# A hybrid encoder block: the planner's prices for TensorE, and small products of two heads in alternation

## The chip, the cores and the metric

One core of a Trainium2 chip runs one transformer-like block on 1024 frames of 1024 channels in float32. The metric is device microseconds of that core for one execution. TensorE (PE) multiplies, VectorE (DVE) and ScalarE (ACT) do elementwise work and empty the PSUM banks, GpSimd (POOL) does little, SyncE (SP) issues every DMA.

## The reference, cut to what matters

```python
h = x
n1 = modulate(rms_norm(h, norm1_g), sh1, sc1)
h = h + 0.5 * g1 * swiglu(n1, ffn1_w1, ffn1_w3, ffn1_w2)
n2 = modulate(rms_norm(h, norm2_g), sh2, sc2)
proj = n2 @ w_in
y_rwkv = rwkv7_mixer(proj[..., :N_RWKV_COLS], ...)      # 8 heads of 64: a recurrent delta rule
y_attn = chunk_band_attention(...)                      # 8 heads of 64: 64-frame chunks, 9-chunk band
h = h + g2 * (concatenate([y_rwkv, y_attn]) @ w_out)
n3 = modulate(rms_norm(h, norm3_g), sh3, sc3)
h = h + 0.5 * g3 * swiglu(n3, ffn2_w1, ffn2_w3, ffn2_w2)
```

The nine vectors sh, sc, g come from `silu(c) @ w_ada + b_ada`. The mixer's in-context rate is `a = sigmoid(a0 + ad @ w_a_up)`, a product over 64 rows: the second product of the low-rank adapters.

## The kernel before, in words

The frames are worked in two halves of 512, A and B. The large products (both feed-forward blocks, the projection, the output projection) take float32 operands split into a high and a low part and make three products of 128 rows, 128 columns and 512 moving columns each, summed in one PSUM bank. Weights stream through `wst` (as they lie in memory), `whi` and `wlo` (high and low part). Tiles of the products are `mm` and `mmb`; the operands are `nh`, `nl` (normed input), `ah`, `al` (gated activations) and `mh`, `ml` (the mixers' outputs).

The order of all instructions is made in Python while the program is built, by a planner. Each stage is a generator that yields what it waits for; `drive` keeps a table of when each engine will be free and each tile ready (class `Clock`) and always resumes the first stage, by priority, that is ready at TensorE's planned time. `mm` and `tp_` (a transpose) tell the table the price `d` of each product on TensorE. On the chip every engine runs its list strictly in that order, and semaphores make it wait where a tile is not there yet. A 512-column product of split operands has the price `n / 2400 + 0.004`, so 0.2173 us; a float32 product of up to 64 columns has `n / 1200 + 0.012`.

The large stages are the mains, in this order of priority: f1A (first feed-forward of half A), pA (projection), oA (output projection), f1B, pB, oB, f2A, f2B. They fill TensorE between the links of the other stages: rA and rB (the recurrence), aA and aB (attention), the norms n1B, n2A, n2B, n3A, n3B, and mA, mB, which read the mixers' outputs back from memory (`mx`), split them and give oA and oB their input. oA waits for rA, aA and pA; pB waits for f1B and oA; n2B waits for f1B. The norms' row factors `rstd`, their `nv` tiles and the `mx` tiles share four buffers named `th`. PSUM has three banks for `mm` and five (pool `b`) for everything else, and a main may take one of the five only when two are free.

The recurrence takes two heads at a time (a pair), four pairs a half, in two groups of two. For each pair `rwkv1` makes the operands: `ap`, the adapter's second product (lines 1203 to 1209), over partitions 64 to 127 only; `gb`, for each head and each of 8 chunks a product of 64 rows by 128 columns by 128 moving columns; and `bt`, 8 transposes a head. Head 0 lies in partitions 0 to 63, head 1 in 64 to 127. All of head 0's `gb` come first, four chunks a bank, then all of head 1's, then `bt` of head 0, then `bt` of head 1. DVE turns each `gb` bank into `GA` and `GR` with a mask. A group's triangular blocks then go through memory to DVE (`inverse`), and `rwkv2` builds two sets of 32-row, 32-column products, `qb` and `ub`, 8 for head 0 and then 8 for head 1, before it walks the 8 chunks with the products `px`, `pu` and `pz`. The output products `yb` follow: first those with `GR`, head by head, then those with `RA` and `Z`, where the code before already alternates the heads, into two banks:

```python
        for c in range(NC):
            for h in range(2):
                s = slice(h * 64, h * 64 + 64)
                self.mm(out(h, c), RA[s, c, 0], Z[s, c], start=False, ...)
```

In the trace a float32 product shows as two matmul records and two weight loads, a transpose and a split-operand product as one of each.

Of the kernel before, what the change touches and what calls it, by code (L numbers as in the profile page):

```python
# [10 lines left out]
AF = mybir.ActivationFunctionType  # L11
# [5 lines left out]
P = 128  # L17
# [5 lines left out]
C = 64  # L23
NC = H // C
# [8 lines left out]
NEVER = 1e9  # L33
# [13 lines left out]
class Clock:  # L47

    SEM = 0.21

    def __init__(self):
        self.pe = 0.0
        self.at = dict(vector=0.0, scalar=0.0, gpsimd=0.0, sync=0.0, dma=0.0)
        self.base, self.wr, self.rd, self.by, self.left = {}, {}, {}, {}, {}
        self.new, self.live = set(), set()
        self.slots, self.psum = {}, set()
# [86 lines left out]
        for x in outs:  # L145
            self.write(x, e, eng)

    def matmul(self, out, ins, d):
        self.pe = max(self.pe, self.after(ins, [out], "pe")) + d
        for x in ins:  # L150
            self.read(x, self.pe + self.SEM)
        self.write(out, self.pe + self.SEM, "pe")

# [86 lines left out]
class Builder:  # L240
    def __init__(self, tc, a, es):
        self.tc, self.a, self.es = tc, a, es
        self.clock = Clock()
        self.nc = Core(tc.nc, self.clock)
        self.uid = 0
        self.tasks, self.mains = [], []
        self.n, self.ssq, self.tags = {}, {}, {}
        self.done, self.group = set(), None

    def nm(self, s):  # L250
        self.uid += 1
# [236 lines left out]
        return self.tile(self.pb, "b", 5, name, reads=reads)  # L488


    def mm(self, out, lhsT, rhs, start=True, stop=True, **kw):
        m, n = width(lhsT), width(rhs)
        if lhsT.dtype == F32R:
            d = n / 2400 + 0.004
        else:
            d = 2 * max(2 * n / 2400, m / 1200) if m > 64 else n / 1200 + 0.012
        self.clock.matmul(out, (lhsT, rhs), d)
        self.nc.tensor.matmul(out, lhsT, rhs, start=start, stop=stop, **kw)  # L498

    def tp_(self, out, in_, ident):  # L500
        self.clock.matmul(out, (in_,), 0.112 if in_.shape[0] > 64 else 0.058)
        self.nc.tensor.transpose(out, in_, ident)  # L502

    def colsum(self, out, x, h=1):
# [220 lines left out]
    def norm(self, key, hf, j, src=None):  # L725
        nc = self.nc
        s = self.sets[hf]
        if j == 0:
            d = 0
            for x in self.fetch(src):  # L730
                if x is None:
                    yield from self.sumsq(hf, j, d, self.fetched)
                    d += 1
                else:
                    yield x
        rstd = yield from self.root(hf, j)
        nh, nl, vs = [], [], []

        def scale(d):
            if j:  # L740
                return getattr(self, f"s{j}")[:, d : d + 1], self.mod[:, 3 * j - 2, d : d + 1]
            return tuple(self.n1m[v][d // 2][:, d % 2 : d % 2 + 1] for v in (1, 0))

        def low(d):
            nc.vector.scalar_tensor_tensor(nl[d], vs[d], scale(d)[1], nh[d].bitcast(F32), op0=OP.add, op1=OP.subtract)

        def step(d, x):
            yield x, rstd, "th", f"n{hf}", lambda: 0.0 if len(self.mains) < 2 else self.clock.at["vector"]
            sc, sh = scale(d)
            v = self.th("nv", 2)  # L750
            nc.vector.scalar_tensor_tensor(v, x, sc, rstd, op0=OP.mult, op1=OP.mult)
            vs.append(v)
            nh.append(self.tile(s, f"n{hf}", 16, "nh", dt=F32R))
            nl.append(self.tile(s, f"n{hf}", 16, "nl", dt=F32R))
            nc.scalar.activation(nh[d], v, AF.Identity, bias=sh)
            if d == 0:
                self.n[key] = nh, nl
            else:
                low(d - 1)

        if src is None:
            for d in range(ND):
                yield from step(d, self.h[hf][d])
                if j == 1:
                    self.free(self.h[hf][d])
        else:
            d = 0
            for x in self.fetch(src):
                if x is None:
                    yield from step(d, self.fetched)  # L770
                    d += 1
                else:
                    yield x
        yield nh[ND - 1]
        low(ND - 1)


    def place(self):
# [387 lines left out]
    def rwkv_prep(self, hf):  # L1166

        nc = self.nc
        lo = yield from self.shift(8, hf)
        gd = yield from self.shift(9, hf)  # L1170
        self.twd = self.tb(hf, "twd")
        self.tad = self.tb(hf, "tad")
        nc.gpsimd.memset(self.twd[64:65], 1.0)
        yield lo
        nc.scalar.activation(self.twd[0:64], lo[0:64], AF.Tanh)
        nc.vector.tensor_copy(self.tad[64:128], lo[64:128])
        self.sgd = self.tb(hf, "sgd")
        yield gd
        nc.scalar.activation(self.sgd, gd, AF.Tanh, scale=0.5)
        self.free(lo, gd)  # L1180
        yield self.sgd
        nc.vector.tensor_scalar(self.sgd, self.sgd, 0.5, 0.5, OP.mult, OP.add)

    def rwkv1(self, hf, p):

        nc = self.nc
        cs = slice(p * P, p * P + P)
        c3 = lambda t: t.rearrange("p (c t) -> p c t", c=NC)
# [3 lines left out]
        nc.sync.dma_start(wdu[0:64], self.a["w_decay_up"][:, cs])  # L1192
        nc.sync.dma_start(wdu[64:65], self.a["w0"][:, cs])
        wau = self.sm("wu", [P, P], 1, reads=1)
        nc.sync.dma_start(wau[64:128], self.a["w_a_up"][:, cs])
        ks = yield from self.shift(4 + p, hf)

# [7 lines left out]

        yield wau, self.tad, "b"
        ap_ = self.bank("ap")
        self.mm(ap_, wau[64:128], self.tad[64:128])
        yield lw
        nc.vector.tensor_scalar(lw, lw, 0.5 * LOGW, 0.5 * LOGW, OP.mult, OP.add)  # L1210

# [37 lines left out]
        RA = self.sm("RA", [P, NC, 2, C], 2)  # L1249
# [18 lines left out]

        GR, GA, BKn = [], [], []
        for h in range(2):  # L1270
            s = slice(h * 64, h * 64 + 64)
            yield f"n{hf}"
            GR.append(self.tb(hf, "GR", [P, NC, C]))
            GA.append(self.tb(hf, "GA", [P, NC, C]))
            for c4 in range(2):
                yield BKB, RA, "b"
                gb = self.bank("gb", 2)
                for i in range(4):
                    c = 4 * c4 + i
                    self.mm(  # L1280
                        gb[:, i * P : i * P + P],
                        BKB[s, c, h : h + 2].rearrange("p k t -> p (k t)"),
                        RA[s, c].rearrange("p k t -> p (k t)"),
                    )
                g4 = gb.rearrange("p (c k t) -> p c k t", c=4, k=2)
                for k, o in ((1, GA[h]), (0, GR[h])):
                    nc.vector.tensor_mul(
                        o[:, 4 * c4 : 4 * c4 + 4], g4[:, :, k],
                        self.gmask[:, k].unsqueeze(1).to_broadcast([P, 4, C]),
                    )  # L1290

        for h in range(2):
            s = slice(h * 64, h * 64 + 64)
            yield BKB, "b", f"n{hf}"
            bt = self.bank("bt")
            for c in range(NC):
                self.tp_(
                    bt[:, c * C : c * C + C],
                    BKB[s, c, h : h + 2].rearrange("p k t -> p (k t)"),
                    self.ident[s, s],  # L1300
                )
            BKn.append(self.tb(hf, "BKn", [P, NC, C]))
            nc.scalar.activation(BKn[h], c3(bt), AF.Copy)
        self.free(BKB)
        yield ks, "b", "bon"
        bon = self.sm("bon", [P, 4, 2], 2, reads=1)
# [3 lines left out]
        i = p % 2  # L1310
# [51 lines left out]
    def rwkv2(self, hf, st):  # L1362
# [17 lines left out]
            nc.vector.transpose(U1[r0], TT[r0, :, 0:32])  # L1380
        yield U1, "b"
        qb = self.bank("qb", 2)
        for h in range(2):
            r0 = slice(h * 64, h * 64 + 32)
            r1 = slice(h * 64 + 32, h * 64 + 64)
            for c in range(NC):
                self.mm(
                    qb[r1, c * 32 : c * 32 + 32], GA[h][r0, c, 32:64], U1[r0, c],
                    tile_position=(h * 64, h * 64 + 32),
                )  # L1390
        yield qb
        for h in range(2):
# [1 line left out]
            nc.scalar.activation(U1[r1], qb[r1, 0:256].rearrange("p (c t) -> p c t", c=NC), AF.Copy)  # L1394
        yield U1, TT, "b"
        ub = self.bank("ub", 2)
        for h in range(2):
            r0 = slice(h * 64, h * 64 + 32)
            r1 = slice(h * 64 + 32, h * 64 + 64)
            for c in range(NC):  # L1400
                self.mm(
                    ub[r0, c * 32 : c * 32 + 32], U1[r1, c], TT[r1, c, 32:64],
                    tile_position=(h * 64 + 32, h * 64),
                )
        self.free(U1)
        yield ub, "tr"
# [40 lines left out]
        nc.sync.dma_start(wgu, self.a["w_g_up"][:, cs])  # L1447
        D_ = self.tr("D", [P, 4, 2, C])
        sm = self.sm("sm", [P, 4, 4, 2], 2)
        yield Z, *UV, lambda: self.clock.freed(self.tags["b"], 1)  # L1450
        yb = [self.bank("yb", 2) for h in range(2)]
        out = lambda h, c: yb[h][c % 2 * 64 : c % 2 * 64 + 64, c // 2 * C : c // 2 * C + C]

# [145 lines left out]
    def run(self):  # L1599
# [28 lines left out]

        self.main("f1A", "n1A", 0, [], self.ffn("n1A", 0, 0, w1, None, hA))
        self.main("pA", "n2A", 1, ["f1A!", "setup2"], self.proj("n2A", 0))  # L1630
        self.main("oA", "mA", 2, ["rA", "aA", "pA!"], self.wout("mA", 0))
        self.main("f1B", "n1B", 3, ["f1A!"], self.ffn("n1B", 1, 0, w1, xB, hB))
        self.main("pB", "n2B", 4, ["f1B!", "oA!"], self.proj("n2B", 1))
        self.main("oB", "mB", 5, ["rB", "aB", "pB!"], self.wout("mB", 1))
# [65 lines left out]
```

## Time and profile before

| | us |
|---|---|
| median of 3 runs (2205.71 to 2212.28) | 2209.58 |
| the profiled execution's own time | 2210.19 |
| its span, first to last instruction | 2208.5 |
| PE busy in the span | 2157.9 (98%) |
| DVE busy | 1465.5 (66%) |
| ACT busy | 900.1 (41%) |
| POOL busy | 127.3 (6%) |

Times in the rows are microseconds from the span's start, unless marked ns. Matmuls overlap in the pipeline, so a record lasts longer (0.39 us for 512 columns) than the distance from its start to the next one's start; the distance is what a product costs. A busy PE is therefore not a PE at its peak.

### The profile page before, as it was taken

Reading aid. Unit: us, or ns where it says so; the run is one execution under the profiler, and the core shown is the slowest. Engines: PE = TensorE matmul, PEld = TensorE weight load, DVE = VectorE, ACT = ScalarE, POOL = GpSimd, SP = SyncE. Lnnn points to the kernel's source line nnn. Section 1 sums busy time; section 2 is a strip of 40 time slices with the busy share of each in tenths; the row PEclk is TensorE's granted clock in tenths of the full one; section 3 lists DMA queues with packets and bytes.
Section 4 is the critical chain, followed back from the end, with each engine's and each line's share of the span. In section 5 each row is a group of like instructions: output and inputs, shape, how many; then the busy total and the mean of one; then the engine's idle time right before and its main releaser. Section 6 shows DMA issues by size and latency. Waiting matters only on the chain.

```text
span 2208.5 us, 32853 instructions
## 1 busy us (share of the span) xinstructions
PE 2157.9 (98%) x11568; PEld 1735.5 (79%) x11568; DVE 1465.5 (66%) x3090; ACT 900.1 (41%) x1712; POOL 127.3 (6%) x156
## 2 busy tenths in 40 slices
PE   7999999999999999999799999999999999999999
PEld 4888887888788778877588788868786787888887
DVE  6877767744578786868664577877886756444444
ACT  4332324445545434333445554435444333233322
POOL 1000000020200000001011300001000000000000
PEclk9999999999999999999899999999999999999999
DMA  7766655436664423333555755424342455433333
GB/s 233 253 198 213 205 144 172 138 114 198 202 189 118 116 75 122 98 96 112 168 172 162 225 153 153 113 81 129 90 126 63 141 164 171 134 99 97 94 97 101
DMA packets 230853, 316.31 MB, mean 143 GB/s; under 512 B 61976, under 2 KB 97824, under 8 KB 230688
## 3 DMA queue, kind: packets, MB, share of 16 engines
q1 hardware_dynamic: 230688, 314.22, 46.8%
q8 instruction: 91, 1.49, 0.3%
q14 instruction: 74, 0.61, 0.1%
HBM read 279.52 MB, written 34.61 MB: 142 GB/s over the span
## 4 chain that ended last, share of the span: by engine, by line
PE 89%; DVE 4%; DMA 3%; SPq 1%; issue 1%; ACT 1%; POOL 0%; DVEq 0%; ACTq 0%
PE mm L498 73%; PE mmb L498 3%; PE yp L498 2%; SPq L166 1%; PE S L498 1%; PE gb L498 1%; PE tr L502 1%; DVE wlo L166 1%; PE cs L502 1%; PE pu L498 1%; PE pz L498 1%; PE px L498 1%; PE yb L498 1%; DMA wa<-in_w_ada 1%; DMA sh<-pT 1%
## 5 line engine op out<-in xcount | busy, mean ns | idle before, releaser
L166 ACT ACTIVATE whi<-wst 128x512 fp32r<-128x512 f32 (+2 forms) x692 | 423.2, 613 | 862.4 <-PE mm L498 705.8
L166 DVE TENSOR_TENSOR wlo<-wst,whi 128x512 fp32r<-128x512 f32 (+2 forms) x692 | 464.7, 675 | 350.7 <-ACT whi L166 328.5
L498 PE MATMUL mm<-nh,whi 128*128 128x512 f32 x1520 | 618.9, 407 | 1.0 <-DVE h L166 1.0
L498 PE MATMUL mm<-nl,whi 128*128 128x512 f32 x1520 | 595.2, 392 | 4.6 <-DVE nl L166 4.6
L498 PE MATMUL mm<-nh,wlo 128*128 128x512 f32 x1520 | 595.9, 392 | 1.5 <-DVE wlo L166 1.3
L498 PEld LDWEIGHTS mm<-nh,wlo 128*128 128x128 f32 x1520 | 286.3, 188 | 64.1 <-DVE wlo L166 2.8
L498 PEld LDWEIGHTS mm<-nh,whi 128*128 128x128 f32 x1520 | 286.6, 189 | 60.8 <-issue 4.6
L498 PEld LDWEIGHTS mm<-nl,whi 128*128 128x128 f32 x1520 | 287.1, 189 | 57.0 <-DVE nl L166 8.5
L498 PE MATMUL mm<-ah,whi 128*128 128x512 f32 x662 | 266.2, 402 | 2.4 <-DVE sw L166 1.5
L498 PE MATMUL mm<-al,whi 128*128 128x512 f32 x662 | 258.4, 390 | 2.7 <-DVE al L166 2.7
L498 PE MATMUL mm<-ah,wlo 128*128 128x512 f32 x662 | 258.4, 390 | 0.0
L166 DVE SCALAR_TENSOR_TENSOR h<-mm,g,h 128x512 f32<-128x512 f32 x181 | 134.4, 746 | 84.6 <-PE mm L498 83.9
L498 PEld LDWEIGHTS mm<-ah,whi 128*128 128x128 f32 x662 | 124.4, 188 | 28.3 <-DVE sw L166 2.1
L498 PEld LDWEIGHTS mm<-al,whi 128*128 128x128 f32 x662 | 124.5, 188 | 26.3 <-DVE al L166 3.9
L498 PEld LDWEIGHTS mm<-ah,wlo 128*128 128x128 f32 x662 | 124.3, 188 | 26.5
L166 ACT ACTIVATE E<-E,st 128x640 f32<-128x640 f32 (+4 forms) x128 | 86.0, 688 | 23.7 <-DVE st L166 22.9
L166 DVE SCALAR_TENSOR_TENSOR acc<-wa,silc,acc 128x512 f32<-128x512 f32 (+1 forms) x120 | 83.5, 706 | 0.6
L166 DVE TENSOR_TENSOR sw<-sw,mm 128x512 f32<-128x512 f32 x84 | 57.8, 688 | 35.4 <-PE mm L498 32.0
L166 ACT ACTIVATE pt<-tr 128x256 fp32r<-128x256 f32 x144 | 49.1, 345 | 67.4 <-PE tr L502 64.2
L498 PE MATMUL mm<-whi,nh 128*128 128x512 f32 x184 | 73.6, 400 | 0.0
L498 PE MATMUL mm<-wlo,nh 128*128 128x512 f32 x184 | 71.8, 390 | 0.0
L498 PE MATMUL mm<-whi,nl 128*128 128x512 f32 x184 | 71.6, 389 | 0.0
(245 smaller groups left out, 2685.6 us busy)
## 6 DMA issues: line engine op xcount, KB each, us to landing
wst<-in_ffn_w SPq DMA_DIRECT2D x468, 256.0 KB, 2.9
wa<-in_w_ada SPq DMA_DIRECT2D x144, 256.0 KB, 4.3
wst<-in_w_v SPq DMA_DIRECT2D x64, 256.0 KB, 2.8
wst<-in_ffn_w SPq DMA_DIRECT2D x64, 192.0 KB, 2.4
wst<-in_w_t SPq DMA_DIRECT2D x40, 256.0 KB, 4.1
wst<-in_w_out SPq DMA_DIRECT2D x32, 256.0 KB, 3.2
kd<-kT SPq DMA_DIRECT2D x48, 128.0 KB, 3.6
bias<-in_bias SPq DMA_DIRECT2D x16, 320.0 KB, 3.5
```

The source lines that it names most:

```text
L166: return f(*args, **kw)
L498: self.nc.tensor.matmul(out, lhsT, rhs, start=start, stop=stop, **kw)
L502: self.nc.tensor.transpose(out, in_, ident)
```

## The change

- The planner's prices change: 0.2270 instead of 0.2173 us for a split-operand product of 512 columns, other values for the small ones, and 0.1 us more whenever a product's rows and columns, rounded up to 32, 64 or 128, differ from those of the product before. `side=2` halves the planned price.
- `gb` and `bt` of the two heads are issued in alternation, each head into its own bank, and the stage waits until two banks of the pool are free. `qb` and `ub` alternate the heads inside the one bank that they had.
- `ap` runs over all 128 rows; GpSimd sets the new half of both operands to zero.
- Only one norm runs at a time (`norming`), and oA may start only when the last unit of f1B has been taken.

```diff
+    TURN = 0.1
...
-    def matmul(self, out, ins, d):
+    def matmul(self, out, ins, d, rows, cols):
+        tiling = tuple(32 if n <= 32 else 64 if n <= 64 else P for n in (rows, cols))
+        if tiling != self.tiling:
+            d += self.TURN
+            self.tiling = tiling
...
+    def two(self):
+        return self.clock.freed(self.tags["b"], 1)
...
         if lhsT.dtype == F32R:
-            d = n / 2400 + 0.004
+            d = max(n / 2400 + 0.0137, 0.111)
+        elif m > 64:
+            d = 2 * max(n / 1200, 0.112)
         else:
-            d = 2 * max(2 * n / 2400, m / 1200) if m > 64 else n / 1200 + 0.012
-        self.clock.matmul(out, (lhsT, rhs), d)
+            d = n / 1200 + 0.005 if m > 1 else n / 600 + 0.005
+        self.clock.matmul(out, (lhsT, rhs), d / side, lhsT.shape[0], m)
...
+        yield lambda: NEVER if self.norming else 0.0
+        self.norming = True
         rstd = yield from self.root(hf, j)
...
+        nc.gpsimd.memset(self.tad[0:64], 0.0)
...
+        nc.gpsimd.memset(wau[0:64], 0.0)
...
-        self.mm(ap_, wau[64:128], self.tad[64:128])
+        self.mm(ap_, wau, self.tad)
...
+        half = [slice(0, 64), slice(64, 128)]
+        for c4 in range(2):
+            yield BKB, RA, self.two
+            gb = [self.bank("gb", 2) for h in range(2)]
+            for i in range(4):
+                c = 4 * c4 + i
+                for h, s in enumerate(half):
                     self.mm(
-                        gb[:, i * P : i * P + P],
+                        gb[h][:, i * P : i * P + P],
                         BKB[s, c, h : h + 2].rearrange("p k t -> p (k t)"),
-                        RA[s, c].rearrange("p k t -> p (k t)"),
+                        RA[s, c].rearrange("p k t -> p (k t)"), side=2,
                     )
...
+        yield BKB, self.two
+        bt = [self.bank("bt") for h in range(2)]
+        for c in range(NC):
+            for h, s in enumerate(half):
+                self.tp_(
+                    bt[h][:, c * C : c * C + C],
+                    BKB[s, c, h : h + 2].rearrange("p k t -> p (k t)"),
+                    self.ident[s, s], side=2,
+                )
...
-        for h in range(2):
-            r0 = slice(h * 64, h * 64 + 32)
-            r1 = slice(h * 64 + 32, h * 64 + 64)
-            for c in range(NC):
+        for c in range(NC):
+            for h in range(2):
+                r0 = slice(h * 64, h * 64 + 32)
+                r1 = slice(h * 64 + 32, h * 64 + 64)
                 self.mm(
                     qb[r1, c * 32 : c * 32 + 32], GA[h][r0, c, 32:64], U1[r0, c],
-                    tile_position=(h * 64, h * 64 + 32),
+                    tile_position=(h * 64, h * 64 + 32), side=2,
                 )
...
-        self.main("oA", "mA", 2, ["rA", "aA", "pA!"], self.wout("mA", 0))
+        self.main("oA", "mA", 2, ["rA", "aA", "pA!", "f1B!"], self.wout("mA", 0))
```

`ub` is changed as `qb` is.

## Rows read from the trace of the kernel before

**Rows 1.** The page: busy time of PE, and the chain that ended last by engine.

```profile
PE 2157.9 (98%) x11568; PEld 1735.5 (79%) x11568; DVE 1465.5 (66%) x3090; ACT 900.1 (41%) x1712; POOL 127.3 (6%) x156
...
PE 89%; DVE 4%; DMA 3%; SPq 1%; issue 1%; ACT 1%; POOL 0%; DVEq 0%; ACTq 0%
```

**Rows 2.** Groups by form, PE: shapes, count, busy us, mean ns of one, idle before.

```profile
L498 PE MATMUL gb<-RA,BKB 64*128 64x128 f32 x256 | 30.2, 280 | 0.0
...
L502 PE MATMUL bt<-ident,BKB 64*128 64x64 f32 x128 | 9.1, 226 | 0.0
...
L498 PE MATMUL ap<-tad,wu 64*128 64x512 f32 x16 | 9.0, 641 | 0.6 <-DVE pt L166 0.6
```

**Rows 3.** Timeline of PE, one pair's gb and bt: start, us, instruction, records.

```profile
649.47 3.16 PE L498 MATMUL gb<-RA,BKB 64*128 64x128 f32 x29
...
652.58 0.27 PE L498 MATMUL gb<-RA,BKB 64*128 64x128 f32 x1
652.60 0.28 PE L502 MATMUL bt<-ident,BKB 64*128 64x64 f32 x2
652.69 0.27 PE L498 MATMUL gb<-RA,BKB 64*128 64x128 f32 x1
652.72 0.74 PE L502 MATMUL bt<-ident,BKB 64*128 64x64 f32 x11
653.39 0.66 PE L502 MATMUL cs<-ident,so 128*128 128x128 f32 x4
```

**Rows 4.** Timeline of PE, one pair's output products, heads in turn in the second line.

```profile
1026.27 1.10 PE L498 MATMUL yb<-UV,GR 128*64 128x64 f32 x32
1027.30 0.69 PE L498 MATMUL yb<-Z,RA 64*64 64x64 f32 x32
```

**Rows 5.** Timeline of PE, one pair's qb and the product behind it.

```profile
753.84 1.09 PE L498 MATMUL qb<-U,GA 32*32 32x32 f32 x32
754.86 0.50 PE L498 MATMUL mm<-nh,whi 128*128 128x512 f32 x1
```

**Rows 6.** Timeline of PE, one pair's ap and the product behind it.

```profile
662.69 1.12 PE L498 MATMUL ap<-tad,wu 64*128 64x512 f32 x2
663.75 0.50 PE L498 MATMUL mm<-nh,whi 128*128 128x512 f32 x1
```

**Rows 7.** Timeline of DVE, first and last of eight mask products of one pair.

```profile
650.66 0.42 DVE L166 TENSOR_TENSOR GA<-gb,gmask 128x256 f32<-128x256 f32 x1 [0.70 <-PE gb L498]
...
653.34 0.41 DVE L166 TENSOR_TENSOR GR<-gb,gmask 128x256 f32<-128x256 f32 x1
```

**Rows 8.** The chain in order of time: start, us, what.

```profile
451.06 2.04 PE mm L498 x9
...
611.53 4.66 DMA sh<-pT
...
1067.77 0.75 DVE nv L166
...
1069.22 0.75 DVE nv L166
```

**Rows 9.** Busy time by stretch: PE, PEld, DVE, ACT, POOL (records), PE's clock, DMA.

```profile
1040.00:1077.00 37.00, 22.76 (x83) 15.74 (x82) 30.67 (x49) 20.28 (x33) 1.01 (x1) 0.80 0.56 199
1825.00:1847.00 22.00, 18.16 (x78) 13.98 (x77) 18.39 (x31) 9.43 (x16) 1.01 (x1) 0.93 0.81 285
...
1062.00:1073.00 11.00, 1.05 (x3) 0.62 (x3) 10.66 (x16) 5.66 (x9) 0.00 (x0) 0.66 0.05 5
```

**Rows 10.** Timeline of SP where oA begins.

```profile
1040.94 0.38 SPq L166 DMA_DIRECT2D mix<-yo  x1
...
1054.13 17.67 SPq L166 DMA_DIRECT2D mx<-mix  x3
```

**Rows 11.** Timeline of PE, the last product of f1B and oA's first after its wait.

```profile
1049.81 0.39 PE L498 MATMUL mm<-ah,wlo 128*128 128x512 f32 x1
...
1072.75 0.79 PE L498 MATMUL mm<-mh,whi 128*128 128x512 f32 x1 [9.95 <-ACT mh L166]
```

More of the change, by code (lines that the diff above doesn't have):

```diff
@@ L51 @@
     SEM = 0.21
+    TURN = 0.1
     def __init__(self):
         self.pe = 0.0
+        self.tiling = None
         self.at = dict(vector=0.0, scalar=0.0, gpsimd=0.0, sync=0.0, dma=0.0)
@@ L248, in __init__ @@
         self.done, self.group = set(), None
+        self.norming = False
     def nm(self, s):
@@ L488, in bank, with mm, tp_ @@
         return self.tile(self.pb, "b", 5, name, reads=reads)
-    def mm(self, out, lhsT, rhs, start=True, stop=True, **kw):
+    def two(self):
+        return self.clock.freed(self.tags["b"], 1)
+    def mm(self, out, lhsT, rhs, start=True, stop=True, side=1, **kw):
         m, n = width(lhsT), width(rhs)
         if lhsT.dtype == F32R:
-            d = n / 2400 + 0.004
-        else:
-            d = 2 * max(2 * n / 2400, m / 1200) if m > 64 else n / 1200 + 0.012
-        self.clock.matmul(out, (lhsT, rhs), d)
+            d = max(n / 2400 + 0.0137, 0.111)
+        elif m > 64:
+            d = 2 * max(n / 1200, 0.112)
+        else:
+            d = n / 1200 + 0.005 if m > 1 else n / 600 + 0.005
+        self.clock.matmul(out, (lhsT, rhs), d / side, lhsT.shape[0], m)
         self.nc.tensor.matmul(out, lhsT, rhs, start=start, stop=stop, **kw)
-    def tp_(self, out, in_, ident):
-        self.clock.matmul(out, (in_,), 0.112 if in_.shape[0] > 64 else 0.058)
+    def tp_(self, out, in_, ident, side=1):
+        self.clock.matmul(out, (in_,), (0.108 if in_.shape[0] > 64 else 0.062) / side, in_.shape[0], P)
         self.nc.tensor.transpose(out, in_, ident)
@@ L775, in norm @@
         low(ND - 1)
+        self.norming = False
     def place(self):
@@ L1270, in rwkv1 @@
         for h in range(2):
-            s = slice(h * 64, h * 64 + 64)
             yield f"n{hf}"
             GR.append(self.tb(hf, "GR", [P, NC, C]))
+            yield f"n{hf}"
             GA.append(self.tb(hf, "GA", [P, NC, C]))
[L1275 to L1279, printed above, removed]
+        half = [slice(0, 64), slice(64, 128)]
[5 more added lines that the diff above has]
+                for h, s in enumerate(half):
                     self.mm(
-                        gb[:, i * P : i * P + P],
+                        gb[h][:, i * P : i * P + P],
                         BKB[s, c, h : h + 2].rearrange("p k t -> p (k t)"),
-                        RA[s, c].rearrange("p k t -> p (k t)"),
+                        RA[s, c].rearrange("p k t -> p (k t)"), side=2,
                     )
-                g4 = gb.rearrange("p (c k t) -> p c k t", c=4, k=2)
+            for h in range(2):
+                g4 = gb[h].rearrange("p (c k t) -> p c k t", c=4, k=2)
                 for k, o in ((1, GA[h]), (0, GR[h])):
@@ L1290, in rwkv1 @@
                     )
-        for h in range(2):
-            s = slice(h * 64, h * 64 + 64)
-            yield BKB, "b", f"n{hf}"
-            bt = self.bank("bt")
-            for c in range(NC):
[L1297 to L1301, printed above, removed]
+        yield BKB, self.two
[7 more added lines that the diff above has]
+                )
+        for h in range(2):
+            yield f"n{hf}"
             BKn.append(self.tb(hf, "BKn", [P, NC, C]))
-            nc.scalar.activation(BKn[h], c3(bt), AF.Copy)
+            nc.scalar.activation(BKn[h], c3(bt[h]), AF.Copy)
         self.free(BKB)
@@ L1382, in rwkv2 @@
         qb = self.bank("qb", 2)
-        for h in range(2):
-            r0 = slice(h * 64, h * 64 + 32)
-            r1 = slice(h * 64 + 32, h * 64 + 64)
-            for c in range(NC):
+        for c in range(NC):
+            for h in range(2):
+                r0 = slice(h * 64, h * 64 + 32)
+                r1 = slice(h * 64 + 32, h * 64 + 64)
                 self.mm(
                     qb[r1, c * 32 : c * 32 + 32], GA[h][r0, c, 32:64], U1[r0, c],
-                    tile_position=(h * 64, h * 64 + 32),
+                    tile_position=(h * 64, h * 64 + 32), side=2,
                 )
@@ L1396, in rwkv2 @@
         ub = self.bank("ub", 2)
[L1397 to L1400, printed above, removed]
+        for c in range(NC):
+            for h in range(2):
+                r0 = slice(h * 64, h * 64 + 32)
+                r1 = slice(h * 64 + 32, h * 64 + 64)
                 self.mm(
                     ub[r0, c * 32 : c * 32 + 32], U1[r1, c], TT[r1, c, 32:64],
-                    tile_position=(h * 64 + 32, h * 64),
+                    tile_position=(h * 64 + 32, h * 64), side=2,
                 )
@@ L1449, in rwkv2 @@
         sm = self.sm("sm", [P, 4, 4, 2], 2)
-        yield Z, *UV, lambda: self.clock.freed(self.tags["b"], 1)
+        yield Z, *UV, self.two
         yb = [self.bank("yb", 2) for h in range(2)]
```

## The prediction

> **What bounds the kernel now.** I read the page first: TensorE (PE) is busy for 98% of the span, and PE carries 89% of the chain that ended last [rows 1]. A product taken off PE is therefore worth its whole distance to the next product, unless something else then ends last. That distance is read from the timeline, not from a record's length: nine split-operand products follow one another in 2.04 us, 0.227 us each [rows 8], though a record of them lasts 0.39 [rows 11]. The groups by form give the number of products that the change touches [rows 2], the timeline of one pair gives what they cost [rows 3, 5, 6], and the stretches show where PE is not filled, which is at the two joins of the halves [rows 9].
>
> **gb and bt in alternation.** The reader should see in rows 3 that head 0 and head 1 run one behind the other: 29 records of gb in 3.16 us, and inside one head a record every 0.11 us (652.58 to 652.69). Where head 1's last gb meets head 0's first bt, the two kinds interleave, and each keeps its own distance (gb 0.11, bt two in 0.12, so 0.06 each): two 64-row products in different halves of the array do not slow each other. Head against head over all 128 columns is what the change does with both. A pair now takes from 649.47 to 653.39, where the next work starts: 3.92 us. In alternation each head has 16 gb records at 0.112 (1.79 us) and 8 bt at 0.0625 (0.50), and the last 0.15 us to the next work stays (the last bt starts at 652.72 + 0.74 - 0.22 = 653.24): 2.44 us. That saves 1.48 us a pair; 256 records of 32 make 8 pairs: 11.8 us. Bounds: nothing, if heads do not overlap, and 3.92 / 2 for 8 pairs, 15.7.
>
> The output products speak for the overlap. 32 records that use two column halves take 1.10 - 0.22 = 0.88 us, and 32 that use two row halves as well take 0.69 - 0.22 = 0.47 [rows 4]; the latter alternate the heads exactly so, into two banks.
>
> **qb and ub in alternation.** 16 products, 32 records, take 1.02 us to the next product, of which the records' starts fill 1.09 - 0.19 = 0.90 [rows 5]. Halved, 0.45 are saved; at the 0.032 that a head's records would need by themselves (0.51 for 16) it is 0.39. I take 0.42, for qb and ub of 8 pairs 16 times: 6.7 us. Bounds: nothing, if two row groups cannot write one bank at once, to 7.2.
>
> A rule speaks against this term. The rows show records 0.47 / 32 = 0.015 us apart [rows 4]. The Trainium skill, page "TensorE: Matmul & The Clock Gate", section "Wait — 56ns, not 53.3ns?", says that starts of matmuls come no closer than about 25 ns, however few columns they move. By it 32 records would need 0.80 us and this term would be 16 x 0.10 = 1.6 us, the whole sum 5.1 us smaller. The trace does not agree for products in different parts of the array, and I go by the trace.
>
> **ap over 128 rows.** Its two records take 1.06 us [rows 6], 0.53 for 512 columns. The trace has no float32 product of 128 rows and 512 columns; the nearest row is gb with 0.112 for 128, so 0.45 for 512. That saves 0.16 us a pair, 1.3 us in all; bounds nothing and, if the two changes of arrangement around it vanish at 0.1 each, 2.9. The two new memsets are GpSimd's, which is busy 6% of the span [rows 1]; what stands behind them on its queue is the next power for a norm's root, and at half a microsecond they cost nothing as long as it is not the last to come. What the wait for two banks can cost is a rival below; while a stage waits, the mains fill PE.
>
> Sum of what leaves PE: 11.8 + 6.7 + 1.3 = 19.8 us, bounds 0 and 25.8.
>
> **The planner's prices.** The old price of a split-operand product is 0.2173 us, measured is 0.227, 4.5% more; changes of arrangement had no price. So on the chip PE has run behind the plan, and links of the recurrence stood in PE's list behind more filler than their wait needed. With true prices fewer products stand between links, and a chain ends earlier against the filler. This matters at the joins. From 1040 to 1077 PE holds 83 records, of which 71 are split-operand products (16.1 us) and 12 small ones (1.3): 19.6 us of 37 are lost, and in 1062 to 1073 almost nothing runs and the granted clock is 0.66, partly at the lower of its two levels [rows 9]. What happens there: the last output of the recurrence is written at 1040.94, f1B's last product starts at 1049.81, and SP's load of `mx` then stands for 17.67 us [rows 10, 11], because n2B's `nv` and `rstd` have taken the `th` buffers. oA has no input for 9.95 us. The second join, 1825 to 1847, loses 22 - 78 x 0.227 = 4.3 us [rows 9].
>
> If mA were through before n2B starts, oA would cover n2B, and the edit that holds oA until f1B is spent keeps that cover. For that the recurrence must end some 12 us earlier against f1B. What pushes: 4.5% of its 430 us (the loads of its first operands land by about 616 [rows 8], the end is at 1041) is 19 us, if PE's list set every link's time; half of it is a fair guess, 10. What pulls: half the 19.8 us leave PE in half A, so f1B's products end 10 us earlier, while the recurrence gains less, since DVE's eight mask products span 650.66 to 653.75 whatever PE does [rows 7]; of 1.48 us a pair perhaps 0.4 reach the chain. With qb, ub and ap I put its gain at 6. Net 10 + 6 - 10 = 6 us of the 12: the join shrinks in part. I take 5 us for both joins together; bounds nothing and 23.9.
>
> The guard on norms costs nothing: by the code n2B follows f1B and n3A follows oA, so two norms meet only if a half overtakes the other.
>
> **Forecast.** 2210.2 (the profiled execution; the median of the runs is 0.6 lower) - 19.8 - 5 = 2185.4, so 2185 us.
>
> **The rivals.**
> - *The join closes.* Both lost stretches go: 2210.2 - 19.8 - 23.9 = 2166. For it speaks that 12 us suffice; against it that both sides move. Chance 0.22.
> - *Half A gives its saving back.* The recurrence keeps its pace, f1B runs out earlier, and PE waits before oA: only half B's 9.9 us and ap's share stay, 2199. DVE's 66% and the mask products speak for it, PE's 89% of the chain against. Chance 0.13.
> - *True prices take away slack (little change).* DVE's nv and nl together repeat every 1.45 us [rows 8]; the planner prices them at 2 x (0.066 + 0.064 + 512 / 960) = 1.33, 8% less. PE running late has hidden that. If each of the 192 bursts of px, pu and pz (8 pairs x 8 chunks x 3) then waits 0.075 us longer, 14 us return: 2199 to 2204 with the joins as they are. Chance 0.08.
> - *Heads do not overlap over full columns.* Then only ap and a part of the joins are left: 2206. Rows 3 and 4 speak against it. Chance 0.05.
> - *Slower: the wait for two banks.* Attention at lower priority takes any single bank that comes free, so a stage that needs two can be passed over. In half A 12 such waits (4 pairs, two gb and one bt) lie on the chain. Each 2.7 us of delay makes 32 us; the chain has 9 us of margin to f1B's end [rows 10, 11], and beyond that PE idles. It decides from about 32 us of delay on; at 45 us the time is 2225. Against it: yb waits for two banks already. Chance 0.07.
> - My forecast: 0.45.
>
> A measurement of this kernel can tell about 0.3%, 6.6 us, from no change. Of the forecast's 0.45 nearly all is beyond that (0.44), of the joins' rival all 0.22, of half A's 0.09, of the others 0.06: faster 0.81. Within: 0.01 + 0.04 + 0.04 + 0.02 = 0.11. Slower: 0.08. The range reaches from the closed joins with a little more saved, 2162, to the rival without overlap, 2205. The forecast's own range is 2174 to 2196.
>
> **What would show it.** In the new trace, gb and bt of an undisturbed pair should take about 2.4 us, in records of both heads 0.007 and 0.105 us apart; qb 0.6 instead of 1.02; ap 0.9. If gb still takes 0.11 us a record through all 32, the overlap is wrong. If these are as said and the span is not 20 us shorter, the time stands as waits of PE before oA or at the links; then the planner's part is wrong. If the stretch without products before oA's rest is gone, the joins were worth more than I gave them.

## The result, and the profile after

The changed kernel takes 2178.68 us (median of 4 runs, 2175.52 to 2181.82) where the kernel before takes 2207.64 in the runs beside it: ratio 0.9864, 95% interval 0.9845 to 0.9882. The forecast was 2185, range 2162 to 2205. The profiled execution took 2181.82 us (span 2180.1), 28.4 less than the one of before (2210.19).

The page, its busy line and the chain that ended last, stands against [rows 1]:

```profile
PE 2136.9 (98%) x11568; PEld 1718.1 (79%) x11568; DVE 1463.8 (67%) x3090; ACT 897.1 (41%) x1712; POOL 128.4 (6%) x166
...
PE 86%; DMA 6%; DVE 4%; ACT 2%; issue 2%; SPq 1%; POOL 0%; DVEq 0%; ACTq 0%; POOLq 0%
```

PE still bounds the kernel, but transfers now have 6% of the chain where they had 3%, a first sign that something of what was won came back as waits for transfers.

The timeline of PE, one pair's gb and bt (against [rows 3]), qb (against [rows 5]) and ap (against [rows 6]):

```profile
862.34 2.06 PE L512 MATMUL gb<-RA,BKB 64*128 64x128 f32 x32
864.33 0.50 PE L512 MATMUL mm<-nh,whi 128*128 128x512 f32 x1
...
865.22 0.71 PE L516 MATMUL bt<-ident,BKB 64*128 64x64 f32 x16
865.86 0.66 PE L516 MATMUL cs<-ident,so 128*128 128x128 f32 x4
...
950.53 0.69 PE L512 MATMUL qb<-U,GA 32*32 32x32 f32 x32
951.16 0.50 PE L512 MATMUL mm<-nh,whi 128*128 128x512 f32 x1
...
842.87 0.39 PE L512 MATMUL mm<-nh,wlo 128*128 128x512 f32 x1
843.10 1.02 PE L512 MATMUL ap<-tad,wu 128*128 128x512 f32 x2
843.56 0.80 PE L512 MATMUL mm<-nh,whi 128*128 128x512 f32 x1
844.20 0.40 PE L512 MATMUL mm<-nl,whi 128*128 128x512 f32 x1
```

From one line's start to the next, gb takes 1.99 us and bt 0.64, together 2.63 for 3.92 before; qb takes 0.63 for 1.02. ap has to be read together with its neighbours, because the product behind it now starts early (0.46 us after ap does) and then takes 0.64. In the kernel before the product ahead of [rows 6] and the one behind them are:

```profile
662.37 0.39 PE L498 MATMUL mm<-nh,wlo 128*128 128x512 f32 x1
...
664.08 0.39 PE L498 MATMUL mm<-nl,whi 128*128 128x512 f32 x1
```

From the product before ap to the second one behind it that is 1.71 us (662.37 to 664.08), and 1.33 after the change (842.87 to 844.20). ap has become shorter, and the 0.32 and 0.33 us that the products on either side of an ap of 64 rows take to the next one, instead of 0.23, are gone.

The timelines of SP and of PE where oA begins (against [rows 10, 11]):

```profile
1022.85 0.38 SPq L172 DMA_DIRECT2D mix<-yo  x1
1023.29 0.92 SPq L172 DMA_DIRECT2D mx<-mix  x2
1025.99 3.57 SPq L172 DMA_DIRECT2D mx<-mix  x3
1031.71 1.52 SPq L172 DMA_DIRECT2D mx<-mix  x3
```

```profile
1047.07 0.39 PE L512 MATMUL mm<-ah,wlo 128*128 128x512 f32 x1
1047.29 0.39 PE L512 MATMUL mm<-mh,whi 128*128 128x512 f32 x1
```

The recurrence of half A writes its last output at 1022.85, 18.1 us earlier than before, and all eight loads of mx are issued by 1033.2, where the last three stood for 17.67 us. In both kernels oA's first product follows f1B's last at 0.22 us, but before the change oA then ran out of `mh` and PE stood for 9.95 us at 1062 [rows 9, 11]; that wait is gone. I call the distance from that write to f1B's last product the margin of join A: it was 8.9 us and is 24.2. Both joins are filled but for 1.5 us, as the busy time by stretch shows (against [rows 9]):

```profile
1010.00:1090.00 80.00, 78.47 (x350) 64.35 (x349) 61.05 (x98) 38.91 (x68) 3.69 (x3) 0.98 0.65 202
1800.00:1850.00 50.00, 50.00 (x223) 41.40 (x222) 23.89 (x38) 15.73 (x27) 0.00 (x0) 1.00 0.47 147
```

The same two stretches of the kernel before had PE busy for 64.94 of 80.00 and 46.16 of 50.00 us, with the granted clock at 0.89 and 0.94.

### The profile page after: what moved, and what is told of

Same layout as the page of the kernel before. It is cut to its first block, busy times and chain, and to the rows that moved or that the text cites. A ratio compares the mean times of both kernels' runs of the same rounds, so it can differ in the third digit from the quotient of the medians.

```text
span 2180.1 us, 32870 instructions
## 1 busy us (share of the span) xinstructions
PE 2136.9 (98%) x11568; PEld 1718.1 (79%) x11568; DVE 1463.8 (67%) x3090; ACT 897.1 (41%) x1712; POOL 128.4 (6%) x166
## 4 chain that ended last, share of the span: by engine, by line
PE 86%; DMA 6%; DVE 4%; ACT 2%; issue 2%; SPq 1%; POOL 0%; DVEq 0%; ACTq 0%; POOLq 0%
PE mm L512 72%; PE mmb L512 3%; PE yp L512 1%; DMA vd<-av 1%; PE tr L516 1%; PE S L512 1%; DMA kd<-kT 1%; SPq L172 1%; PE cs L516 1%; DVE wlo L172 1%; PE gb L512 1%; PE pu L512 1%; DMA wst<-in_ffn_w 1%; PE px L512 1%; PE pz L512 1%
## 5 line engine op out<-in xcount | busy, mean ns | idle before, releaser
L512 PE MATMUL mm<-ah,whi 128*128 128x512 f32 x670 | 273.3, 408 | 2.1 <-ACT ah L172 1.2
```

## The experiments

All were timed against the kernel before, on the same chip as it, in five rounds. The kernel before took between 2207.6 and 2210.5 us in these comparisons, so a difference between the medians of two experiments is good to some 3 us. "Plan" means the order of every engine's list.

**1. The same plan, one head behind the other.** The planner sees the alternation, but within each burst head 0's products are handed out first.

```diff
+    def one_by_one(self):
+        for go in self.held[0::2] + self.held[1::2]:
+            go()
+        self.held = []
```

> The plan of the changed kernel, every list of every engine as there, but within each burst of gb, bt, qb and ub head 0's products are issued first and then head 1's. Theory (overlap of two row groups is what pays): gb, bt, qb and ub give back about 18 us, so some 2196 us against 2179; a burst of 16 gb records takes 1.8 us instead of 0.9. Rival (the alternation is worth little, the time came from the new order of everything else): within 5 us of the changed kernel, 2174 to 2184.

Measured: 2195.03 us, ratio to before 0.9931 (0.9916 to 0.9946). The order on the other engines is that of the changed kernel, so 2195.0 - 2178.7 = 16.3 us are what the overlap on PE is worth (14.8 by the two ratios to the kernel before). Its timeline of PE shows the same bursts:

```profile
871.05 2.82 PE L513 MATMUL gb<-RA,BKB 64*128 64x128 f32 x32
873.79 0.50 PE L513 MATMUL mm<-nh,whi 128*128 128x512 f32 x1
...
874.70 1.02 PE L528 MATMUL bt<-ident,BKB 64*128 64x64 f32 x16
875.65 0.66 PE L528 MATMUL cs<-ident,so 128*128 128x128 f32 x4
...
961.40 1.09 PE L513 MATMUL qb<-U,GA 32*32 32x32 f32 x32
962.42 0.50 PE L513 MATMUL mm<-nh,whi 128*128 128x512 f32 x1
```

gb takes 2.74 us for 1.99, bt 0.95 for 0.64 and qb 1.02 for 0.63. For 8 pairs, each with a qb and a ub, these lines make 8 x (3.69 - 2.63) + 16 x 0.39 = 14.7 us. A gb burst is not twice as long; probably a few records still overlap where one head follows the other, as at the border of gb and bt in [rows 3]. The rival, within 5 us, is refuted; the other half of the change, plan and ap, is worth 2209.8 - 2195.0 = 14.8 us.

**2. The old prices.** Alternation, ap and the other edits as in the changed kernel.

```diff
-        tiling = tuple(32 if n <= 32 else 64 if n <= 64 else P for n in (rows, cols))
-        if tiling != self.tiling:
-            d += self.TURN
-            self.tiling = tiling
...
-            d = max(n / 2400 + 0.0137, 0.111)
+            d = n / 2400 + 0.004
...
-            d = n / 1200 + 0.005 if m > 1 else n / 600 + 0.005
+            d = n / 1200 + 0.012
...
```

> The changed kernel with the planner's old prices for products and no price for a change of arrangement; alternation (side=2), ap over 128 rows, the guard on norms and oA's wait stay. Theory (prediction: 19.8 us leave PE, some 9 come from the plan's joins): 2188 to 2190 us, and the stretch without products before oA's rest is there again, some 10 us or more. Rival (prices do nothing, alternation alone shortens the joins too): 2179 within 4 us.

Measured: 2191.35 us, 0.9913 (0.9899 to 0.9927). The margin is -2.2 us (last output at 1039.05, f1B's last product at 1036.89) and the join is open again: PE is busy for 62.27 of 80.00 us from 1010 to 1090. The time lies 1.4 us above the range of the theory, the join is as the theory said, and the rival, within 4 us of 2179, is refuted. The prices are worth 12.7 us on top of the alternation, and they, not the alternation, brought the recurrence forward: without them f1B's end moved by 12.9 us and the recurrence's by only 1.9, so that the margin shrank from 8.9 to -2.2.

**3. The prices alone.** The products head by head, priced in full, and ap over 64 rows, under the new planner.

```diff
-        for c4 in range(2):
-            yield BKB, RA, self.two
-            gb = [self.bank("gb", 2) for h in range(2)]
+            for c4 in range(2):
+                yield BKB, RA, "b"
+                gb = self.bank("gb", 2)
...
-        self.mm(ap_, wau, self.tad)
+        self.mm(ap_, wau[64:128], self.tad[64:128])
```

> The kernel before with the new prices, the guard on norms and oA's wait alone: gb, bt, qb, ub head by head as before and priced in full, ap over 64 rows. Theory: 8 to 10 us faster than before, 2198 to 2200, from the joins. Rival (true prices take the slack that hid late operands): 2208 or more.

Measured: 2193.29 us, 0.9928 (0.9908 to 0.9948): 16.5 us less than before, where 8 to 10 were expected. The margin is 34.6 us (1018.36 to 1053.00), PE is busy for all of 1010 to 1090 and of 1800 to 1850. The rival is refuted.

**4. Transfers that land later in the plan.**

```diff
-            e = self.at["dma"] + 0.9
+            e = self.at["dma"] + 2.4
```

> The changed kernel with 1.5 us more for the landing of every transfer in the planner's table (2.4 instead of 0.9 us behind the transfer itself). In the changed kernel's chain transfers have 6% where they had 3% before. Theory (what was won at the joins was partly returned as waits for transfers that the plan thinks landed): 3 to 10 us faster than the changed kernel, fewer waits of PE behind vd and kd. Rival (the waits come from the queue's order, or are hidden): within 3 us, or slower since stages start later.

Measured: 2171.93 us, 0.9828 (0.9815 to 0.9841), 6.8 us faster than the changed kernel, within the theory's 3 to 10, although join A is open again. SP's timeline is that of the kernel before once more, with the last loads of mx standing for 17.25 us:

```profile
1026.38 0.38 SPq L172 DMA_DIRECT2D mix<-yo  x1
...
1040.14 17.25 SPq L172 DMA_DIRECT2D mx<-mix  x3
```

The margin is 9.3 us. Most of PE's waits in the attention are gone: from 500 to 1800 the three below made 9.3 us in the changed kernel, and 2.0 of them are left here, as the list of waits says (who waited for whom, us in total, times, longest), first of the changed kernel:

```profile
PE yp L512 <- DVE pt L172: 4.3, 8, 1.4
PE tr L516 <- ACT E L172: 3.0, 8, 0.6
PE yp L512 <- ACT pt L172: 2.0, 1, 2.0
```

and of this one:

```profile
PE mm L512 <- ACT mh L172: 11.2, 2, 10.0
...
PE yp L512 <- DVE pt L172: 2.0, 3, 1.4
```

The wait for `mh` is join A. The same list for ACT points to where those in the attention come from. These are its waits for the transfers of `vd` and `kd` (values and keys), in the kernel before, the changed one and this one:

```profile
ACT V L166 <- DMA vd<-av: 10.9, 10, 1.8
ACT K L166 <- DMA kd<-kT: 6.5, 6, 4.3
...
ACT V L172 <- DMA vd<-av: 23.5, 11, 3.7
ACT K L172 <- DMA kd<-kT: 13.1, 8, 3.2
...
ACT V L172 <- DMA vd<-av: 4.1, 3, 2.1
ACT K L172 <- DMA kd<-kT: 3.1, 5, 1.0
```

They make 17.4 us before, 36.6 in the changed kernel and 7.2 here.

**5 and 6. n2B behind mA**, with the old prices and with the late transfers.

```diff
-        go("n2B", lambda: self.norm("n2B", 1, 1), 1, ["f1B", "fin107"])
+        go("n2B", lambda: self.norm("n2B", 1, 1), 1, ["f1B", "fin107", "mA"])
```

> The kernel with the old prices and the alternation, in which the norm n2B starts only when mA has read and split all of oA's input. With the old prices mA's last loads stood behind n2B's buffers and 1000 to 1100 lost some 18 us. Theory (the join costs what it does because n2B takes the th buffers before mA is through): oA covers n2B, 8 to 12 us less than with the old prices alone, 2179 to 2184 us. Rival (PE waits for the end of the recurrence anyway): within 4 us of 2191.

> The changed kernel with 1.5 us more for the landing of transfers in the plan, and n2B behind mA. That kernel alone took 2172 us although the join was back (some 20 us lost from 1000 to 1100, the last three loads of mx standing for 17.25 us). Theory as for the kernel with old prices: 8 to 14 us less, 2158 to 2164, the fastest here. Rival: the recurrence's end decides, within 4 us of 2172.

Measured: 2181.05 us, 0.9859 (0.9842 to 0.9876), 10.3 less than experiment 2; and 2159.25, 0.9766 (0.9752 to 0.9780), 12.7 less than experiment 4. Both hit. The margins are the same as without the edit (-2.2 and 9.3), so what was won back had been lost because n2B took the `th` buffers, not because the recurrence ended late. It is not the whole loss: from 1010 to 1090 PE still stands for 11.4 us of 17.7 in 5, and for 5.1 of 14.6 in 6. In the changed kernel mA is through before n2B anyway, and the edit makes no difference to any list.

**7. VectorE 8% dearer in the plan.**

```diff
-                d = 0.066 + 0.064 * ptr + n / (1920 if fast else 960)
+                d = 1.08 * (0.066 + 0.064 * ptr + n / (1920 if fast else 960))
```

> The changed kernel with VectorE's operations 8% dearer in the plan, as measured for nv and nl. Theory of the prediction's rival (true prices of TensorE took away slack that hid VectorE's cheap prices): at least 4 us faster than 2179. Against it: within 4 us, or slower because links are issued later.

Measured: 2198.95 us, 0.9951 (0.9936 to 0.9966), 20 us slower than the changed kernel. The margin is 2.3 us (1049.25 to 1051.58) and both joins are open: 63.69 of 80.00 and 43.26 of 50.00 us. The theory, at least 4 us faster, is refuted as a whole: with VectorE dearer the recurrence is planned later, and the joins open. Whether VectorE's cheap prices hold PE up elsewhere it does not settle: outside the joins, in 500 to 1000 and 1100 to 1750 together, PE stands for 12.3 us here and for 16.0 in the changed kernel.

**8 and 9. No price for a change of arrangement**, alone and with n2B behind mA.

```diff
-    TURN = 0.1
+    TURN = 0.0
```

> The changed kernel without the price for a change of arrangement (0 instead of 0.1 us), all other new prices kept. Theory (the products' own prices move the recurrence against the filler, the turn's price adds to it): some 4 us slower than 2179, the join partly back. Rival (the turn's price is what did it): 8 us or more slower, as with all old prices, 2187 to 2192.

> The changed kernel without the price for a change of arrangement, and n2B behind mA. Without that price the last output of half A's recurrence was written at 1043.79 (1022.85 in the changed kernel), the last loads of mx stood behind n2B, 1000 to 1100 lost 25.7 us and 1800 to 1900 10.1. Theory (that meeting is the loss): 12 to 18 us less than 2208, 2190 to 2196; what is left over 2179 is the second join. Rival (late recurrence costs the time by itself): within 5 us of 2208.

Measured: 2207.63 us, 0.9986 (0.9973 to 0.9998), 29 us slower than the changed kernel; and 2195.09, 0.9928 (0.9910 to 0.9946). The margin is 1.4 us in both. My theory for 8 missed: without the turn's price the products' new prices do not bring the recurrence forward against f1B (the last output at 1043.79, against 1039.05 in experiment 2, the margin 1.4 against -2.2). The rival named the right part of the change and set its worth too low. For 9 the theory hit in the time: 12.5 us of the loss are the meeting of n2B and mA. But what is left is not only the second join: from 1010 to 1090 PE still stands for 8.8 us, and for 6.7 from 1800 to 1850.

**10. Only the price for a change of arrangement.** The old prices of products, with TURN at 0.1.

```diff
-            d = max(n / 2400 + 0.0137, 0.111)
+            d = n / 2400 + 0.004
...
-            d = 2 * max(n / 1200, 0.112)
+            d = 2 * max(2 * n / 2400, m / 1200)
...
-            d = n / 1200 + 0.005 if m > 1 else n / 600 + 0.005
+            d = n / 1200 + 0.012
...
```

> The changed kernel with the old prices of products but with 0.1 us for a change of arrangement. Theory (the turn's price alone brings the recurrence forward): the last output of half A's recurrence before 1028, time 2175 to 2183. Rival (both prices are needed): after 1035, 2188 us or more.

Measured: 2158.32 us, 0.9762 (0.9743 to 0.9780), with experiment 6 the fastest kernel here, 20 us under the changed one. The last output is written at 1020.84, as the theory said, and the margin is 17.8 us; the time is 17 us below the theory's range. PE is busy for all of 1010 to 1090 and of 1800 to 1850. Its page, and f1B's last product on PE:

```profile
PE 91%; DVE 3%; DMA 3%; issue 1%; SPq 1%; ACT 0%; DVEq 0%; ACTq 0%
```

```profile
1038.64 0.39 PE L512 MATMUL mm<-ah,wlo 128*128 128x512 f32 x1
```

f1B ends 8.4 us earlier than in the changed kernel, with the same products to do, and transfers are back at 3% of the chain. A table of the two kinds of price (us):

| | no price for a turn | 0.1 us a turn |
|---|---|---|
| old prices of products | 2191.35 | 2158.32 |
| new prices of products | 2207.63 | 2178.68 |

The turn's price saves 33.0 or 29.0 us, and the new prices of products, taken together, cost 16.3 or 20.4.

**11. Transfers that land 2.5 us later in the plan**, n2B behind mA.

> The changed kernel with 2.5 us more for the landing of transfers in the plan (3.4 instead of 0.9), and n2B behind mA. Theory (waits for transfers are what is left in the attention): within 4 us of the 2159 us at 2.4, since medians of landing are 2.4 to 4.3 us. Rival (a later plan starts its stages too late): 2165 or more.

The edit is that of 4 with 3.4 for 2.4, and that of 6. Measured: 2188.50 us, 0.9900 (0.9883 to 0.9918). The rival hit: the recurrence's last output is written at 1051.5, 20 us after f1B's last product, and from 1010 to 1090 PE stands for 19.7 us although n2B comes behind mA.

**12. The old price of split-operand products alone**, everything else as in the changed kernel.

```diff
-            d = max(n / 2400 + 0.0137, 0.111)
+            d = n / 2400 + 0.004
```

> The changed kernel with one price as before: a split-operand product at n / 2400 + 0.004 (0.2173 us for 512 columns), all other new prices and the turn's price kept. Theory (the cheap filler is the slack that hides late transfers of the attention, and the turn's price alone brings the recurrence forward): as with the turn's price alone, 2155 to 2163, and yp, tr and the short S cost some 8 us less than in the changed kernel. Rival (the prices of the small products do it): 2173 or more.

Measured: 2191.74 us, 0.9914 (0.9896 to 0.9931). A miss: not 2155 to 2163; the rival, 2173 or more, hit. The margin is 5.5 us and the join open, as SP's timeline shows:

```profile
1037.22 0.81 SPq L172 DMA_DIRECT2D mix<-yo  x1
...
1049.32 17.98 SPq L172 DMA_DIRECT2D mx<-mix  x4
```

So the price of the filler (the split-operand products) is not what cost 20 us between the changed kernel and experiment 10. On the contrary: this run and the changed kernel differ in that price alone, and with the new one the last output comes at 1022.85 instead of 1037.22, the join shuts, and 13.1 us are saved. The small products' new prices are what costs: this run and experiment 10 differ in them alone, by 33.4 us. Which of them it is, is open, and so is what the new price of the filler does beside the old ones of the small products.

Without the condition that oA waits for f1B's last unit, or without the guard on norms, the planner makes the same lists for every engine; these edits are worth nothing here and were not run. The wait for two banks was not tried by itself.

## Why the prediction was right, and where it was not

**gb and bt.** Right. Forecast 2.44 us a pair, found 2.63, probably since the two groups now stand apart with filler between them and each pays its own way out. (3.92 - 2.63) x 8 = 10.3 us for the 11.8 forecast.

**qb and ub.** Right: 0.39 us a burst for the 0.42 taken, 6.2 us for 6.7. 32 records start within 0.69 - 0.19 = 0.50 us, 0.016 apart, two row groups of one bank included. The rule of the Trainium skill ("TensorE: Matmul & The Clock Gate", section "Wait — 56ns, not 53.3ns?") that starts come no closer than about 25 ns does not hold here for products in different parts of the array; the trace decides. The cause is shown by experiment 1: with every list of the plan held fixed, one head behind the other costs 16.3 us by the medians and 14.8 by the ratios, and 14.7 by the lines of its own bursts.

**ap.** 1.71 - 1.33 = 0.38 us for a pair whose ap stands between split-operand products, so some 3 us if all eight are like it, for the 1.3 forecast. That is the forecast's upper bound, 2.9: the two changes of arrangement around ap vanish, which I had left out of the sum.

**The joins.** This is the step that was mis-sized: "I take 5 us for both joins together". They closed, which I had as a rival at 2166 with a chance of 0.22. The mechanism was as stated: n2B's tiles stand in `th`, SP's loads of mx behind them, PE without input (experiments 5, 6 and 9). The first error is in "Net 10 + 6 - 10 = 6 us of the 12": the margin grew by 15.3 us, from 8.9 to 24.2. Without the new prices it shrinks by 11.1 (experiment 2), with them and without the alternation it grows by 25.7 (experiment 3); I had these two at -4 and +10. The second error is to take a part of the gain for a part of the way, for the loss is nearly a step. With n2B free to start:

| kernel or experiment | margin, us | PE stands from 1010 to 1090, us |
|---|---|---|
| 2 | -2.2 | 17.7 |
| 8 | 1.4 | 16.5 |
| 7 | 2.3 | 16.3 |
| 12 | 5.5 | 16.5 |
| before | 8.9 | 15.1 |
| 4 | 9.3 | 14.6 |
| 10 | 17.8 | 0.0 |
| 1 | 22.3 | 1.3 |
| changed | 24.2 | 1.5 |
| 3 | 34.6 | 0.0 |

The edge lies somewhere between 9.3 and 17.8. With n2B behind mA there is no such step, but the end of the recurrence still costs: PE stands for 5.1 us at a margin of 9.3 (6), 8.8 at 1.4 (9), 11.4 at -2.2 (5) and 19.7 where the last output comes 20 us after f1B's last product (11).

**Why the recurrence ended earlier.** The prices did it (experiments 2 and 3), but my reason for it was at best a part. I gave the credit to the true price of the split-operand products, 4.5%, and only a sentence to the changes of arrangement. With the old prices of products the price of a turn alone brings the last output from 1039 to 1021 (experiments 2 and 10), and without it the new prices bring nothing (8). The true price of the split-operand products does bring the recurrence forward beside the turn's price and the new small ones (12 against the changed kernel), but the new prices of products as a whole cost 16 to 20 us. So the sign came out right, and the sum behind it did not. Each set of prices was one plan, and neighbouring sets differ by up to 33 us either way; how much of that belongs to a price and how much to the one plan that came of it is not shown.

**What was returned.** 28.4 us were gained in the profiled execution; 10.3, 6.2 and 3.0 of direct savings and the joins' 19.6 and 4.3 would be 43.4. Some 15 were returned, which I had not put in the sum. So that the time came within 7 us of my forecast is luck: the joins gave 19 more than I took for them, and 15 of it was lost again. A good half of the 15 shows as PE standing in half B, from 1100 to 1750: 4.6 us before, 12.8 in the changed kernel, 1.0 in experiment 4 and 3.0 in experiment 10. Where the rest lies is not shown. My rival of lost slack named VectorE, which experiment 7 does not settle. What ACT's waits and experiment 4 point to is transfers, and ACT's list behind them. The changed kernel's timeline of ACT, and of PE just then:

```profile
1238.28 0.63 ACT L172 ACTIVATE K<-kd 128x512 fp32r<-128x512 f32 x1 [3.18 <-DMA kd<-kT]
1238.94 0.60 ACT L172 ACTIVATE pev<-mm 128x512 f32<-128x512 f32 x1
1239.43 0.62 ACT L172 ACTIVATE whi<-wst 128x512 fp32r<-128x512 f32 x1
1239.95 0.38 ACT L172 ACTIVATE pt<-tr 128x256 fp32r<-128x256 f32 x1
```

```profile
1240.38 0.39 PE L512 MATMUL yp<-pt,V 128*128 128x256 f32 x1 [2.00 <-ACT pt L172]
```

ACT stands 3.18 us for a transfer of the next head's keys; the `pt` that PE needs is three places behind it. The changed kernel's page has a median of 3.9 us from issue to landing for `kd`, where the plan's formula gives 1.1 + 0.37 + 0.9 = 2.4 for its 128 KB on an idle queue. Pricing the landing 1.5 us later takes most such waits away (experiment 4), 2.5 us later loses more at the join than it saves (experiment 11).

**Half A gives its saving back, two banks, no overlap.** None decided the time: join A is shut, and the bursts overlap over full columns. But the first was right in its mechanism: with the alternation and the old prices (experiment 2) f1B runs out 12.9 us earlier, the recurrence gains 1.9, and only the new prices cover it.

## What to carry to other kernels

Small products that sit in different row groups of the array should be issued in turn: at a fixed plan that was worth some 15 us here, bursts that took 1.4 to 1.6 times as long head by head, for the price of a loop's order. Where a list is made by a planner, look first for the events to which it gives no price or a much too small one (a change of arrangement, a transfer's real landing). Exact prices for what it already sees are no safe gain: together they cost 16 to 20 us here, though one of them saved 13. So time each price by itself, and look at the order that comes of it. And where two stages share buffers at a join, ask which comes first and by how much: the loss was a step here, and an explicit order (n2B behind mA) took two thirds of the loss away at a margin of 9.3 us and a third at -2.2.

## What the runs showed of the hardware that was not expected

A wait of PE was paid for again afterwards. Busy time by stretch of the changed kernel around the wait above (PE, PE's clock, DMA), and PE's timeline behind it:

```profile
1237.00:1241.00 4.00, 1.76 (x7) 1.00 0.48 152
1241.50:1245.70 4.20, 4.20 (x18) 0.62 0.64 178
```

```profile
1241.85 0.39 PE L512 MATMUL mm<-nl,whi 128*128 128x512 f32 x1
1242.08 0.39 PE L512 MATMUL mm<-nh,wlo 128*128 128x512 f32 x1
...
1243.39 0.63 PE L512 MATMUL mm<-nl,whi 128*128 128x512 f32 x1
1243.82 0.63 PE L512 MATMUL mm<-nh,wlo 128*128 128x512 f32 x1
```

PE is idle for 2.2 of 4 us at a granted clock of 1.00, and in the 4.2 us behind it the clock is 0.62, so mostly at the lower of its two levels, 1.2 GHz. A split-operand product then takes 0.43 us to the next one (1243.39 to 1243.82), where it took 0.23 just before (1241.85 to 1242.08).

A float32 product of 512 columns was slower over 64 rows than over 128. Where the next product does not start early, the two records of ap take 0.86 us to it over 128 rows (671.17 to 672.03), and 1.06 over 64 [rows 6]:

```profile
671.17 1.02 PE L512 MATMUL ap<-tad,wu 128*128 128x512 f32 x2
672.03 0.27 PE L516 MATMUL tr<-ident,E 128*128 128x128 f32 x1
```
